# The FFN input product by a Strassen scheme of seven half-token products, and weight tiles moved by 192 bytes

## The chip, the cores and the metric

The kernel runs on one core of one Trainium2 chip. The metric is the device time of one execution in microseconds (us). Engines are named as in the profile: PE is TensorE (its weight loads are listed as PEld), DVE is VectorE, ACT is ScalarE, POOL is GpSimd, SP is the engine that issues the DMAs. All of the data is fp32; matmuls read it as fp32r, in three products of split operands (below).

## The reference

512 tokens of width 1024 pass through eight mixer and FFN blocks: two layers of the form FFN, mixer (an mLSTM in the first, a windowed attention in the second), FFN, with a layer norm after each, and then two layers of a gated mixer and an FFN, with an RMS norm ahead of each. Six FFNs are computed in all, each with 2816 hidden units:

```python
def swiglu(x, w_in, w_out):
    gu = x @ w_in                              # 512 x 1024 by 1024 x 5632
    g, u = gu[..., :D_FF], gu[..., D_FF:]      # D_FF = 2816
    return (jax.nn.silu(g) * u) @ w_out        # 2816 -> 1024
```

The change touches `x @ w_in` in each of these six.

## The kernel before

Activations lie transposed: eight tiles of 128 features by 512 tokens (`xh`, `xl`: the fp32r rounding of x, and the rest). Every weight tile is split in the same way, by `split` (L171 to L177): ACT writes the rounding `wh` (L174), DVE subtracts it from the raw tile and writes `wl` (L177). `mm3` (L202 to L208) then makes a product of three matmuls: x high by w high (L206), x low by w high (L207), x high by w low (L208). Each matmul has a weight load of its own. The weight is the stationary operand (128 by 128), x is the moving one (512 columns, or 256 where tokens are taken by halves HA and HB).

`raw` (L179) loads a weight tile of 128 by 1024 (512 KB) into a ring of three (`wr`); `wh` and `wl` have rings of three as well. All of these tiles start at multiples of 256 bytes within a partition, since `fill` tiles pad the pools to that.

`ffn` (L272) has 22 pairs of hidden tiles, `w_in[m, :, j]` with j = 0 for g and j = 1 for u; one `w_in` tile holds all of K = 1024 for 128 hidden units. `pre` (L216) takes the first four tiles (m = 0, 1), half of the tokens at a time, so that it can begin while the norm before it still works on HB. The norm's work on a half is a generator that `flush(s.start)` (L224) empties ahead of the half's matmuls. `gemms` (L231) then takes the other 40 tiles with 512 moving columns, 24 matmuls a tile, two weight tiles ahead. `gate` (L279 to L284) follows each pair: ACT's silu of g (L281), DVE's product with u (L283), and the split of the result into `hh`, `hl` for the second matmul. `out_gemm` multiplies by `w_out`: `out_head` (L323) takes whole rows of 512 tokens in units of eight, eight and six k-tiles, `out_tail` the last rows by halves, and the norm that follows begins inside that.

The order of instructions in an engine's queue is not that of the program text: the framework's scheduler lays them out when the kernel is built, each engine taking the earliest instruction in the text that is ready by then. The rings and the data set what is ready.

Of the kernel before, what the change touches and what calls it, by code (L numbers as in the profile page):

```python
# [34 lines left out]
AP, AF_, AK = 2, 3, 1  # L35
NP = 4
PACE = 2.0
# [19 lines left out]
class Core:  # L57
    def __init__(self, ctx, tc, consts):
# [127 lines left out]
    def weights(self, src, n=1024, at=None):  # L186

        w = self.raw(src, n)
        if at:
# [12 lines left out]
    def mm3(self, out, w, k, xh, xl, start, stop):  # L202
        mm = self.nc.tensor.matmul
        wh, wl = (a[k // 4][:, k % 4 * 128:k % 4 * 128 + 128] if isinstance(a, tuple) else a[:, k * 128:(k + 1) * 128]
                  for a in w)
# [9 lines left out]

    def pre(self, srcs, ats=()):  # L216

# [53 lines left out]

    def ffn(self, w_in, w_out, half, post, tail=None):  # L272

        nc, tc = self.nc, self.tc
        with tc.tile_pool(name="h", bufs=1) as hp:
            hh = [hp.tile([128, T], F32R, name=f"hh{m}") for m in range(NM)]
            hl = [hp.tile([128, T], F32R, name=f"hl{m}") for m in range(NM)]

            def gate(m, pg, pu):  # L279
                sg = hp.tile([128, T], F32, name="sg", bufs=2)  # L280
                nc.scalar.activation(sg, pg, AF.Silu)  # L281
                hf = hp.tile([128, T], F32, name="hf", bufs=2)
                nc.vector.scalar_tensor_tensor(hf, pu, half, sg, op0=OP.mult, op1=OP.mult)  # L283
                self.split(hh[m], hl[m], hf)  # L284
            first = [(m, j) for m in range(3) for j in range(2)][:NP]
            ats = [tuple(tuple(a[m:m + 2]) for a in (hh, hl)) for m in range(NM - 2, NM - 2 * (NP - 2), -2)]
            p0 = dict(zip(first, self.pre([w_in[m, :, j] for m, j in first], ats)))
            pend = {}

            def cb(m, j):  # L290
                def f(p):
                    pend[j] = p
                    if j:
                        gate(m, pend[0], p)
                return f
            for (m, j), p in p0.items():
                cb(m, j)(p)
            self.run((self.gemms([("a", w_in[m, :, j], cb(m, j)) for m in range(NM) for j in range(2)
                                  if (m, j) not in p0]), 1.0))
            self.out_gemm(w_out, hh, hl, NM, post, tail or FT)  # L300

    def out_gemm(self, w_out, hh, hl, nk, post, tail):

        self.run((self.out_head(w_out, hh, hl, nk, post, KD - tail), 1.0))
        self.out_tail(w_out, hh, hl, nk, post, tail)
# [16 lines left out]

    def out_head(self, w_out, hh, hl, nk, post, head):  # L323
        post.begin(self)
        seq = [(d, (i, min(i + 8, nk))) for d in range(head) for i in range(0, nk, 8)]
        held = {}
        for i, u in enumerate(seq):
# [3 lines left out]
            if i == len(seq) - 1:  # L331
                self.first_tail(w_out, nk, head)
            d, (k0, k1) = u
            if k0 == 0:
                p = self.bank()
# [1184 lines left out]
def program(tc, d, out):  # L1520
    with ExitStack() as ctx:
# [11 lines left out]
        with tc.tile_pool(name="b2t", bufs=1) as S:  # L1533
            c.fill(S, 1216)
# [8 lines left out]
        for l in range(2):  # L1543
            w = {n: d["b_" + n][l] for n in ("hf", "hq", "hg", "c", "hi", "nq", "kk", "vv", "w1", "out", "rope")}
            b2.layer(l, w, RMS(c.k("ffn_g", 8 * l, 8)))
            c.ffn(d["b_win"][l], d["b_wout"][l], 1.0, Out(out) if l else RMS(c.k("mix_g", 8, 8)))

# [127 lines left out]
```

## Time and profile before

| | us |
|---|---|
| median of three runs | 3350.05 (3348.68 to 3352.29) |
| profiled execution, its own time | 3350.13 |
| span of its instructions | 3348.3 |
| PE busy | 3305.9 (99%) |
| DVE busy | 1686.3 (50%) |
| ACT busy | 1280.9 (38%) |
| mean of the DMA queues | 91 GB/s |

A busy time is the sum of an engine's instructions. Matmuls are pipelined, so one that lasts 0.39 us may be followed by the next 0.227 us after its start; the pace is read from starts. In the lists below a row has the start, the time it lasts, the engine, the line, the operation with its tiles (out <- in), and how many were merged into the row. What stands in brackets is the engine's idle time before it and what ended that.

### The profile page before, as it was taken

What the parts mean: (1) busy time and instruction counts of PE and PEld (TensorE: products, weight loads), DVE (VectorE), ACT (ScalarE), POOL (GpSimd) and SP (SyncE); (2) the same over time, 40 slices, a digit from 0 to 9 for tenths busy, and PEclk for the clock granted to TensorE, in tenths of its full rate; (3) what the DMA queues carried; (4) which work ended last, traced back from release to release, by engine and by line L of the source; (5) the groups of instructions that cost most, each with busy time, mean ns of one, the idle gap of its engine ahead of it and who ended that gap; (6) DMA issues with size and microseconds to landing.
All of it is one profiled execution on the core that took longest, in us unless ns stands there. A gap on an engine that the chain in (4) does not pass through costs nothing.

```text
span 3348.3 us, 46248 instructions
## 1 busy us (share of the span) xinstructions
PE 3305.9 (99%) x18704; PEld 2827.0 (84%) x18704; DVE 1686.3 (50%) x3451; ACT 1280.9 (38%) x2231; POOL 96.1 (3%) x138
## 2 busy tenths in 40 slices
PE   8999999999999999999999989999999999999999
PEld 7888977988898888879888978788888988898888
DVE  4333756733354333787334667775333567853332
ACT  3322545522233222685222433563232335632221
POOL 0000011000000000110000000000000000000000
PEclk9999999999999999999999989999999999999999
DMA  4333322233332333212333523112333332023333
GB/s 143 96 94 97 100 76 64 89 97 98 93 109 89 100 94 108 74 41 89 95 98 98 163 88 94 45 51 82 99 95 94 107 115 64 26 72 102 98 101 95
DMA packets 88918, 304.04 MB, mean 91 GB/s; under 512 B 9857, under 2 KB 12417, under 8 KB 88705
## 3 DMA queue, kind: packets, MB, share of 16 engines
q1 hardware_dynamic: 88704, 301.10, 29.3%
q8 instruction: 146, 2.39, 0.3%
q14 instruction: 68, 0.55, 0.0%
HBM read 298.96 MB, written 2.10 MB: 90 GB/s over the span
## 4 chain that ended last, share of the span: by engine, by line
PE 94%; DVE 3%; ACT 2%; DMA 1%; issue 1%; POOL 0%; DVEq 0%; SPq 0%; ACTq 0%; POOLq 0%
PE b L206 26%; PE b L208 26%; PE b L207 26%; PE b L267 2%; PE b L268 2%; PE b L266 2%; PE b L1250 1%; PE b L1442 1%; PE b L1391 1%; PE b L1420 1%; PE b L716 1%; ACT wh L174 1%; DVE wl L177 1%; PE b L1303 1%; DMA wr<-w_in 1%
## 5 line engine op out<-in xcount | busy, mean ns | idle before, releaser
L174 ACT ACTIVATE wh<-wr 128x1024 fp32r<-128x1024 f32 (+3 forms) x532 | 545.0, 1026 | 1568.1 <-PE b L207 980.5
L177 DVE TENSOR_TENSOR wl<-wr,wh 128x1024 fp32r<-128x1024 f32 (+3 forms) x532 | 628.3, 1183 | 867.2 <-ACT wh L174 864.9
L206 PE MATMUL b<-xh,wh 128*128 128x512 f32 (+1 forms) x2712 | 1021.7, 378 | 9.5 <-ACT xh L174 7.4
L208 PE MATMUL b<-xh,wl 128*128 128x512 f32 (+1 forms) x2712 | 1008.8, 373 | 3.2 <-DVE wl L177 3.2
L207 PE MATMUL b<-xl,wh 128*128 128x512 f32 (+1 forms) x2712 | 1008.7, 373 | 2.9 <-DVE xl L177 1.8
L206 PEld LDWEIGHTS b<-xh,wh 128*128 128x128 f32 x2712 | 511.1, 189 | 105.5 <-issue 9.4
L208 PEld LDWEIGHTS b<-xh,wl 128*128 128x128 f32 x2712 | 512.5, 189 | 94.5 <-DVE wl L177 5.8
L207 PEld LDWEIGHTS b<-xl,wh 128*128 128x128 f32 x2712 | 513.1, 189 | 91.7 <-issue 3.5
L206 PE MATMUL b<-hh,wh 128*128 128x512 f32 (+1 forms) x1144 | 400.4, 350 | 0.0
L208 PE MATMUL b<-hh,wl 128*128 128x512 f32 (+1 forms) x1144 | 398.4, 348 | 0.0
L207 PE MATMUL b<-hl,wh 128*128 128x512 f32 (+1 forms) x1144 | 398.3, 348 | 0.0
L283 DVE SCALAR_TENSOR_TENSOR hf<-b,sg 128x512 f32<-128x512 f32 x132 | 90.7, 691 | 407.4 <-PE b L208 404.0
L206 PEld LDWEIGHTS b<-hh,wh 128*128 128x128 f32 x1144 | 216.5, 189 | 28.6 <-issue 1.0
L207 PEld LDWEIGHTS b<-hl,wh 128*128 128x128 f32 x1144 | 216.5, 189 | 28.5 <-issue 1.0
L208 PEld LDWEIGHTS b<-hh,wl 128*128 128x128 f32 x1144 | 216.5, 189 | 27.6
L267 PE MATMUL b<-wl,xh 128*128 128x512 f32 (+2 forms) x352 | 122.8, 349 | 4.3 <-DVE wl L177 4.2
L266 PE MATMUL b<-wh,xh 128*128 128x512 f32 (+2 forms) x352 | 125.1, 360 | 0.0
L268 PE MATMUL b<-wh,xl 128*128 128x512 f32 (+2 forms) x352 | 122.7, 349 | 0.0
L177 DVE TENSOR_TENSOR hl<-hf,hh 128x512 fp32r<-128x512 f32 x132 | 89.9, 685 | 0.0
L174 ACT ACTIVATE hh<-hf 128x512 fp32r<-128x512 f32 x132 | 82.8, 632 | 0.8
L1395 ACT ACTIVATE sc<-sc,nm 128x128 f32<-128x128 f32 (+3 forms) x128 | 71.1, 557 | 23.5 <-DVE nm L1393 22.5
L267 PEld LDWEIGHTS b<-wl,xh 128*128 128x128 f32 x352 | 67.2, 191 | 14.3 <-DVE wl L177 6.1
(408 smaller groups left out, 4122.1 us busy)
## 6 DMA issues: line engine op xcount, KB each, us to landing
wr<-w_in SPq DMA_DIRECT2D x176, 512.0 KB, 3.7
wr<-b_win SPq DMA_DIRECT2D x88, 512.0 KB, 3.7
wr<-w_out SPq DMA_DIRECT2D x80, 512.0 KB, 3.5
wr<-b_wout SPq DMA_DIRECT2D x36, 512.0 KB, 3.5
wr<-w_out SPq DMA_DIRECT2D x36, 384.0 KB, 3.1
wr<-b_out SPq DMA_DIRECT2D x20, 512.0 KB, 3.6
wr<-b_w SPq DMA_DIRECT2D x16, 512.0 KB, 3.8
wr<-b_wout SPq DMA_DIRECT2D x16, 384.0 KB, 3.2
```

The lines of the kernel that those rows point to most:

```text
L174: nc.scalar.activation(h, src, AF.Copy)
L177: nc.vector.tensor_sub(l, src, h.bitcast(F32))
L206: mm(out, wh, xh, start=start, stop=False)
L207: mm(out, wh, xl, start=False, stop=False)
L208: mm(out, wl, xh, start=False, stop=stop)
L266: mm(ps[t][:, :n], self.xh[k][:, ts], wh, start=k == 0, stop=False)
L267: mm(ps[t][:, :n], self.xh[k][:, ts], wl, start=False, stop=False)
L268: mm(ps[t][:, :n], self.xl[k][:, ts], wh, start=False, stop=k == KD - 1)
L283: nc.vector.scalar_tensor_tensor(hf, pu, half, sg, op0=OP.mult, op1=OP.mult)
L716: nc.tensor.matmul(p[:, :257], w[:, (j - j0) * 128:(j - j0 + 1) * 128], v[s][:, h], start=s == ss[0], stop=s == ss[-1])
L1250: nc.tensor.matmul(p[:, i * 64:(i + 1) * 64], K[h][:, ts], q, start=True, stop=True)
L1395: nc.scalar.activation(sc[:, :N], sc[:, :N], AF.Exp, bias=nm[:, g:g + 1], scale=-1.0, accum_out=sm[:, g:g + 1])
```

## The change

Two things change. `ffn` computes the input product of hidden pairs 1 to 10 (a pair is m = 2p and 2p + 1, with its g and its u) by a Strassen-Winograd scheme. K and the tokens are halved, and g and u are the two rows of blocks: seven products stand for eight. One product is `w` (128 hidden units twice, K = 512) by x (K = 512, 256 tokens), 2 x 4 x 3 matmuls of 256 columns, in one PSUM bank. Pair 0 stays with `pre`. The stationary operands of three products are sums of weight blocks, which DVE makes from the raw tiles (`weight`). The moving ones of four products are differences of x blocks (`stage`, made once for each FFN, ahead of `pre`'s HB half; in the last two FFNs x is first put together from `xh + xl` by `whole`). The results are put together in `after`, by DVE adds from PSUM. h stays in fp32 for each pair, and is split for the second matmul at the end (`halves`). Weight reads go over seven raw tiles (three of the ring and four more), in the order of use, with two runs of 2 KB for each partition.

And the rings `wr`, `wh`, `wl` begin 192 bytes past a multiple of 256; 64 bytes behind them bring everything after back to a multiple.

In the diff, `ks` in `stage` are four pieces of 256 columns (one of 1024 in the last two FFNs, `normed`), `put` is a `split` of 1024, `b` in `after` is the product's bank (128 by 512), `whole` is eight adds of 256 for each half where `normed`, and `halves` makes one split of 1024 for each pair of hidden tiles.

```diff
         self.act = ctx.enter_context(tc.tile_pool(name="act", bufs=1))
+        self.fill(ctx.enter_context(tc.tile_pool(name="fill0", bufs=1)), 192)
         self.wraw = ctx.enter_context(tc.tile_pool(name="wraw", bufs=3))
         self.wsp = ctx.enter_context(tc.tile_pool(name="wsp", bufs=3))
+        self.fill(ctx.enter_context(tc.tile_pool(name="fill1", bufs=1)), 64)
...
         for s in (HA, HB):
             self.flush(s.start)
+            if then:
+                then(s)
...
+            def stage():
...
+                for k in ks:
+                    sub(q("t1", k), g("b11", k), g("b12", k))
+                for k in ks:
+                    sub(q("t3", k), g("b22", k), g("b12", k))
+                for k in ks:
+                    stt(q("t2", k), q("t1", k), -1.0, g("b22", k), op0=OP.mult, op1=OP.subtract)
+                put("t2")
+                for k in ks:
+                    stt(q("t4", k), q("t2", k), -1.0, g("b21", k), op0=OP.mult, op1=OP.subtract)
+                put("t3")
+                put("t1")
...
+            def weight(st):
+                p, x = st
+                g = lambda q: raws[p, q]
+                if x == "p6":
+                    held["s2", p] = wide("s2", dt=F32)
+                    nc.vector.tensor_add(held["s2", p], g(0), g(3))
+                elif x == "p5":
+                    nc.vector.tensor_add(g(2), g(2), g(3))
...
+                self.split(wh, wl, src)
+                if x == "p2":
+                    nc.vector.tensor_add(g(0), g(0), g(2))
+                elif x == "p7":
+                    nc.vector.tensor_add(g(1), g(1), held.pop(("s2", p)))
...
+            def product(st, w):
+                p, x = st
+                P[x] = self.bank()
+                for m in range(2):
+                    for k in range(4):
+                        wk = tuple(a[:, m * T + k * 128:m * T + k * 128 + 128] for a in w)
+                        self.mm3(P[x][:, m * 256:m * 256 + 256], wk, None, *moving(x, k), k == 0, k == 3)
...
+            def after(st):
...
+                if x == "p1":
...
+                    nc.scalar.activation(A[p], b, AF.Copy)
+                elif x == "p2":
...
+                    add(G[p], A[p], b)
+                    nc.scalar.activation(G[p], G[p], AF.Silu)
+                elif x == "p6":
+                    add(A[p], A[p], b)
+                elif x == "p7":
...
+                    add(V[p], A[p], b)
+                elif x == "p5":
...
+                    add(A[p], A[p], b)
+                    add(U[p], V[p], b)
+                elif x == "p3":
...
+                    add(a, a, b)
+                    nc.scalar.activation(a, a, AF.Silu)
+                    nc.vector.scalar_tensor_tensor(pairs(h[p])[:, :, HB], pairs(u), -half, pairs(a), op0=OP.mult,
+                                                   op1=OP.mult)
+                elif x == "p4":
...
+                    add(v, v, b)
+                    nc.vector.scalar_tensor_tensor(pairs(h[p])[:, :, HA], pairs(v), -half, pairs(G.pop(p)), op0=OP.mult,
+                                                   op1=OP.mult)
+            steps = [(p, x) for p in (1, 2) for x in ("p1", "p2")]
+            steps += [(p, x) for p in (1, 2) for x in ("p6", "p7", "p5", "p3", "p4")]
+            steps += [(p, x) for p in range(3, NP2) for x in ("p1", "p2", "p6", "p7", "p5", "p3", "p4")]
...
+            def then(s):
+                whole(s)
+                if s is HB:
+                    fetch()
+                    ahead(0, 2)               # weight() of the first two steps
+                    stage()
...
+            for i, st in enumerate(steps):
+                ahead(i, 3)
+                product(st, ready.popleft())
+                after(st)
+                if i == len(steps) - 3:
+                    loaded[units[0]] = self.out_load(w_out, units[0])
+                    halves(5)
+                elif i == len(steps) - 2:
+                    loaded[units[1]] = self.out_load(w_out, units[1])
+                    halves(9)
```

## Rows read from the trace of the kernel before

**Rows 1.** The page, parts 1 and 4: busy times, and the chain that ended last.
```profile
PE 3305.9 (99%) x18704; PEld 2827.0 (84%) x18704; DVE 1686.3 (50%) x3451; ACT 1280.9 (38%) x2231; POOL 96.1 (3%) x138
...
PE 94%; DVE 3%; ACT 2%; DMA 1%; issue 1%; POOL 0%; DVEq 0%; SPq 0%; ACTq 0%; POOLq 0%
```
**Rows 2.** Table by stretch, the third FFN's input: busy of each engine, clock, DMA share, GB/s.
```profile
1018.00:1237.00 219.00, 218.47 (x964) 180.48 (x963) 78.26 (x84) 65.76 (x86) 0.00 (x0) 1.00 0.33 101
```
**Rows 3.** PE in order of time, 512 columns: the first and last of 28 matmuls.
```profile
1039.83 0.39 PE L207 MATMUL b<-xl,wh 128*128 128x512 f32 x1
...
1045.95 0.39 PE L207 MATMUL b<-xl,wh 128*128 128x512 f32 x1
```
**Rows 4.** PE in order of time, 256 columns (`pre`): first and last of 11 matmuls.
```profile
1016.81 0.28 PE L207 MATMUL b<-xl,wh 128*128 128x256 f32 x1
...
1018.01 0.28 PE L208 MATMUL b<-xh,hl 128*128 128x256 f32 x1
```
**Rows 5.** PE in order of time, the second and third matmul of `gemms`.
```profile
1018.58 0.40 PE L207 MATMUL b<-xl,wh 128*128 128x512 f32 x1
...
1019.50 0.50 PE L208 MATMUL b<-xh,wl 128*128 128x512 f32 x1 [0.53 <-DVE wl L177]
```
**Rows 6.** Groups by line and form, DVE and ACT: busy, mean ns | idle before.
```profile
L177 DVE TENSOR_TENSOR wl<-wr,wh 128x1024 fp32r<-128x1024 f32 x466 | 570.4, 1225 | 845.3 <-ACT wh L174 843.2
L283 DVE SCALAR_TENSOR_TENSOR hf<-b,sg 128x512 f32<-128x512 f32 x132 | 90.7, 691 | 407.4 <-PE b L208 404.0 <-ACT sg L281 3.4
...
L174 ACT ACTIVATE wh<-wr 128x1024 fp32r<-128x1024 f32 x466 | 493.1, 1060 | 1424.1 <-PE b L207 884.3 <-issue 435.0 <-PE b L268 64.8
```
**Rows 7.** DVE in order of time, with no idle time between: starts give the pace.
```profile
1019.36 1.28 DVE L283 SCALAR_TENSOR_TENSOR hf<-b,sg 128x512 f32<-128x512 f32 x2
1020.56 1.22 DVE L177 TENSOR_TENSOR wl<-wr,wh 128x1024 fp32r<-128x1024 f32 x1
1021.69 1.29 DVE L177 TENSOR_TENSOR hl<-hf,hh 128x512 fp32r<-128x512 f32 x2
1022.90 1.22 DVE L177 TENSOR_TENSOR wl<-wr,wh 128x1024 fp32r<-128x1024 f32 x1
```
**Rows 8.** DVE in order of time in a layer norm's loop over d.
```profile
985.28 0.42 DVE L464 TENSOR_TENSOR x<-x,b 128x256 f32<-128x256 f32 x1 [2.77 <-PE b L405]
985.74 0.42 DVE L465 TENSOR_TENSOR x<-x,b 128x256 f32<-128x256 f32 x1
986.08 0.41 DVE L464 TENSOR_TENSOR x<-x,b 128x256 f32<-128x256 f32 x1
...
986.86 0.42 DVE L464 TENSOR_TENSOR x<-x,b 128x256 f32<-128x256 f32 x1
987.52 0.42 DVE L471 TENSOR_TENSOR xl<-x,xh 128x256 fp32r<-128x256 f32 x1 [0.24 <-ACT x L469]
```
**Rows 9.** ACT and DVE in order of time: the first weight split of `gemms`.
```profile
1017.13 1.06 ACT L174 ACTIVATE wh<-wr 128x1024 fp32r<-128x1024 f32 x1 [3.50 <-PE b L207]
...
1018.22 1.23 DVE L177 TENSOR_TENSOR wl<-wr,wh 128x1024 fp32r<-128x1024 f32 x1 [4.13 <-ACT wh L174]
```
**Rows 10.** DVE in order of time, the same place in the first and fifth FFN.
```profile
34.27 1.23 DVE L177 TENSOR_TENSOR wl<-wr,wh 128x1024 fp32r<-128x1024 f32 x1 [12.29 <-ACT wh L174]
...
2301.97 1.23 DVE L177 TENSOR_TENSOR wl<-wr,wh 128x1024 fp32r<-128x1024 f32 x1 [10.18 <-ACT wh L174]
```
**Rows 11.** PE in order of time: ten transposes of 128 columns, and the matmul behind.
```profile
1504.28 1.31 PE L911 MATMUL b<-ident,sc 128*128 128x128 f32 x10
1505.35 0.48 PE L206 MATMUL b<-q,wh 128*128 128x512 f32 x1
```
**Rows 12.** The page, part 5: the counts of matmuls with a weight of the ring.
```profile
L206 PE MATMUL b<-xh,wh 128*128 128x512 f32 (+1 forms) x2712 | 1021.7, 378 | 9.5 <-ACT xh L174 7.4
...
L206 PE MATMUL b<-hh,wh 128*128 128x512 f32 (+1 forms) x1144 | 400.4, 350 | 0.0
```

More of the change, by code (lines that the diff above doesn't have):

```diff
@@ L188, in weights @@
         w = self.raw(src, n)
-        if at:
+        if at and not isinstance(at[0], tuple):
+            h, l = at
+            self.split(h[:, :n], l[:, :n], w[:, :n])
+        elif at:
             for i in range(0, n, T):
@@ L270, in gemms, with ffn @@
                 j[3](ps)
-    def ffn(self, w_in, w_out, half, post, tail=None):
+    def ffn(self, w_in, w_out, half, post, tail=None, normed=False):
         nc, tc = self.nc, self.tc
+        NP2 = NM // 2
         with tc.tile_pool(name="h", bufs=1) as hp:
[L276 to L300, printed above, removed]
@@ L302, in out_gemm, with wide, whole @@
-    def out_gemm(self, w_out, hh, hl, nk, post, tail):
-        self.run((self.out_head(w_out, hh, hl, nk, post, KD - tail), 1.0))
+            def wide(name, bufs=1, dt=F32R):
+                return hp.tile([128, 1024], dt, name=name, bufs=bufs)
+            h = [None] * NP2
+            form, staged = {}, {}
+            parts = {"b11": (0, HA), "b12": (0, HB), "b21": (4, HA), "b22": (4, HB)}
+            def whole(s):
+                for i, n in enumerate(parts):
+                    k0, t = parts[n]
+                    if normed and t is s:
+                        staged[n] = wide(f"h{1 + i}", dt=F32)
+                        for k in range(4):
+                            nc.vector.tensor_add(staged[n][:, k * 256:k * 256 + 256], self.xh[k0 + k][:, t].bitcast(F32),
+                                                 self.xl[k0 + k][:, t].bitcast(F32))
@@ new lines, in moving @@
+            def moving(n, k):
+                if n in ("p1", "p2"):
+                    k, s = (k, HA) if n == "p1" else (k + 4, HA)
+                elif n in ("p3", "p4"):
+                    k, s = (k + 4, HB) if n == "p3" else (k, HB)
+                else:
+                    a, b = form[{"p5": "t1", "p6": "t2", "p7": "t3"}[n]]
+                    return a[:, k * 256:k * 256 + 256], b[:, k * 256:k * 256 + 256]
+                return self.xh[k][:, s], self.xl[k][:, s]
+            loads = deque((p, q) for ps in [(1, 2)] + [(p,) for p in range(3, NP2)] for qs in ((0, 1), (2, 3))
+                          for p in ps for q in qs)
@@ new lines, in ffn, with fetch @@
+            slots, raws, n = [None] * 7, {}, [0]
+            def fetch():
+                while loads:
+                    i = n[0] % 7
+                    if slots[i] is not None:
+                        return
+                    p, q = slots[i] = loads.popleft()
+                    w = self.wraw.tile([128, 1024], F32, name="wr") if i < 3 else wide("er", 4, F32)
+                    j, r = divmod(q, 2)
+                    nc.sync.dma_start(w.rearrange("p (m c) -> p m c", m=2),
+                                      w_in[2 * p:2 * p + 2, :, j, r * T:r * T + T].rearrange("m p c -> p m c"))
+                    raws[p, q] = w
+                    n[0] += 1
@@ new lines, in ffn, with ahead @@
+            steps = [(p, x) for p in (1, 2) for x in ("p1", "p2")]
+            steps += [(p, x) for p in (1, 2) for x in ("p6", "p7", "p5", "p3", "p4")]
+            steps += [(p, x) for p in range(3, NP2) for x in ("p1", "p2", "p6", "p7", "p5", "p3", "p4")]
+            ready = deque()
+            def ahead(i, k):
+                while len(ready) < k and i + len(ready) < len(steps):
+                    ready.append(weight(steps[i + len(ready)]))
+            def then(s):
+                whole(s)
+                if s is HB:
+                    fetch()
+                    ahead(0, 2)
+                    stage()
@@ new lines, in ffn @@
+            ats = [(wide(f"h{i}"), wide(f"h{i - 1}")) for i in (10, 8, 6)]
+            ps = self.pre([w_in[m, :, j] for m in range(2) for j in range(2)], ats, then)
+            for k in range(4):
+                self.split(self.xh[k][:, HB], self.xl[k][:, HB], staged["t4"][:, k * 256:k * 256 + 256])
+            hh, hl = [], []
+            pair = wide("hh0"), wide("hl0")
+            for m in range(2):
+                sg = hp.tile([128, T], F32, name="ga", bufs=2)
+                nc.scalar.activation(sg, ps[2 * m], AF.Silu)
+                nc.vector.scalar_tensor_tensor(sg, ps[2 * m + 1], half, sg, op0=OP.mult, op1=OP.mult)
+                for a, o in zip(pair, (hh, hl)):
+                    o.append(a[:, m * T:m * T + T])
+                self.split(hh[m], hl[m], sg)
@@ new lines, in ffn, with halves @@
+            names = [None, "t2h", "t2l", "t3h", "t3l", "t1h", "t1l", "s2"] + ["er"] * 4
+            def halves(k):
+                while len(hh) <= k:
+                    p = len(hh) // 2
+                    a = [wide(n, 4 if n == "er" else 1) for n in (names[p], names[11] if p == 1 else f"h{p - 1}")]
+                    self.split(*a, h[p])
+                    for i, o in zip(a, (hh, hl)):
+                        o.extend(i[:, m * T:m * T + T] for m in range(2))
+            units = [(0, (i, min(i + 8, NM))) for i in (0, 8)]
@@ new lines, in ffn @@
+            loaded = {}
+            for i, st in enumerate(steps):
[8 more added lines that the diff above has]
+                    halves(9)
+            self.out_gemm(w_out, hh, hl, NM, post, tail or FT, loaded, halves)
@@ L305, in out_gemm @@
+    def out_gemm(self, w_out, hh, hl, nk, post, tail, loaded=None, need=None):
+        self.run((self.out_head(w_out, hh, hl, nk, post, KD - tail, loaded, need), 1.0))
         self.out_tail(w_out, hh, hl, nk, post, tail)
```

57 lines of the change are left out of this document (50 added, 7 removed).

## The prediction

> **What bounds the kernel now.** I read the page first. PE is busy for 99% of the span and holds 94% of the chain that ended last; DVE and ACT hold 3% and 2% [rows 1]. So time goes only where PE does less, or waits. Next I took the stretch that is replaced, in the table by stretch. In the third FFN's input PE is busy 218.5 of 219 us, at a granted clock of 1.00 (the 2.4 GHz level), DVE 78 us, ACT 66 us, and the DMA share is 0.33 [rows 2]; the other five look alike. Busy time tells no pace, since matmuls overlap, so I took starts. Matmuls of 512 columns start (1045.95 - 1039.83) / 27 = 0.2267 us apart [rows 3], those of 256 columns (1018.01 - 1016.81) / 10 = 0.120 us apart [rows 4]. Both are 13 ns above what their columns need at 2.4 GHz (213.3 and 106.7 ns). So two matmuls of half the tokens cost 0.240 us for one of 0.2267, and part of what seven for eight gives is lost at once.
>
> **PE's work.** A pair takes 4 tiles x 24 = 96 matmuls of 512 columns before: 96 x 0.2267 = 21.76 us. After, 7 x 24 = 168 of 256 columns: 168 x 0.120 = 20.16 us. That is 1.60 us a pair, and 96.0 us for 10 pairs in 6 FFNs. Matmuls grow by 720 an FFN, to 18704 + 4320 = 23024. The rest (`pre`, `w_out`, the mixers) keeps its count.
>
> The Trainium skill ("TensorE: Matmul & The Clock Gate", Back-to-back issue gap) gives a start-to-start gap of N / 2.4 + 2.5 ns, which would be an estimated 215.8 and 109.2 ns, 2.4 us a pair and 142 us in all. The trace differs, with 226.7 and 120.0, and the sum goes by the trace.
>
> **DVE's work, which is what grows.** Starts with no idle time between give DVE's pace: 1.13 us for 1024 columns, 0.60 for 512 [rows 7], 0.34 for 256 [rows 8]. I take the adds at the price of the subtractions of the same width; the evacuating adds at that of the gate's product, which reads PSUM too and lasts 0.691 [rows 6]. A pair now has seven splits and four weight adds of 1024, and nine operations of 512: 11 x 1.13 + 9 x 0.60 = 17.83 us, 88% of PE's 20.16 (before, 36% [rows 2]). ACT has ten operations, of at most 1.06 us each [rows 6], 10.6 us. So DVE fits, with 2.3 us to spare, if its queue is filled well. A weight tile's slot comes free when its product ends, two products (5.76 us) before the tile that takes the slot is wanted; a split takes 1.06 + 0.03 + 1.23 us [rows 9], with an add ahead some 1.2 more. That fits too.
>
> The queue's order decides. In the text, DVE waits for ACT in the middle of p6, p5 and p3 (an add, then ACT, then DVE again). But the queue isn't in the text's order. In the norm's loop the text has L464, L465, L471 for each d; DVE ran L464 of the third d ahead of the first L471 [rows 8], and between the gate's product and `hl` it ran a whole `wl` [rows 7]. Such waits get filled with other ready work, and I take them at nothing. If they aren't filled, see the second rival.
>
> **The start of each FFN.** Three FFNs follow a layer norm's last tail. There DVE has an idle time of 4.13 us ahead of the first `wl` [rows 9], so it is free 4.0 us before `pre` ends. Into the queue come two splits and an add (3.4), `stage` with 16 x 0.34 + 3 x 1.13 = 8.8, the splits of t4 (1.4) and pair 0's gate (2.4): 16.0 us. With two pairs, whose first two splits and add are counted, DVE has 16.0 + 35.7 - 3.4 = 48.3 us to do, less 4.0 ahead: 44.3 against PE's 40.3. PE must wait at least 4 us; in the text's order 10 (below). I take 6, nearer to the lower end as rows 8 show a filled queue: 18 us for three. The two FFNs behind an RMS norm have 10.2 us of idle time, the first FFN 12.3 [rows 10]. For the former 2.7 us of `whole` come on top and `stage` is 0.9 shorter: 48.3 + 1.8 - 10.1 = 40.0, so 0 to 6; I take 1.5, twice. The first: 0 to 2, I take 0.5. Together 21.5 us. Something comes back: `gemms` began with a wait for `wl`, 0.92 us between starts where 0.23 is the pace [rows 5]. The first weights are now split before `pre` ends, so 0.69 x 6 = 4.1 us are won.
>
> **The end of each input product.** Ten splits of h (11.3 us), four of `w_out` (4.5) and six evacuations (3.6) come into the last three products and the first two units of `w_out`: 19.4 us in 8.6 + 48 x 0.2267 = 19.5. It just fits. Between 0 and two late splits (2.3 us); I take 0.5, for six FFNs 3 us. DMA moves the same bytes in 7% less time, at a share of 0.33 [rows 2], with seven raw tiles ahead: nothing, unless a tile lands more than a pair late.
>
> **The offset.** No row shows a weight tile off a multiple of 256, so I bound it. In `pre` the pace is the same 0.120 whether the weight is of the ring or of an h tile (`hl`, the last of rows 4). The nearest floor is ten transposes of 128 columns, a weight load each, at (1505.35 - 1504.28) / 10 = 0.107 us [rows 11]. So at most 13 ns a matmul are to be won, on all that have a weight of the ring; and I let as much be lost, with less right, since no steady stretch that I read has more than 13 ns over the columns. I take zero.
>
> The Trainium skill ("SBUF — State Buffer", Who interferes with whom) says that PE has two independent read ports, for weights and for moving data, and waits on nobody; by that the offset would do nothing. No run here shows it yet.
>
> **Sum.** -96.0 - 4.1 + 21.5 + 3 = -75.6 us. Against the profiled execution's own 3350.13 (span 3348.3; the median of the runs, 3350.05, is the same) that gives 3275. With the ends of the start and end costs alone the same case reaches from 3262 to 3310.
>
> **Rivals.**
> *The offset takes off part of the 13 ns.* For it: both widths have the same excess, so it hangs on the matmul and its weight load, not on the columns, and transposes run without it [rows 11]. Against it: it is there with any weight tile. In full, 168 x 0.107 = 18.0 us a pair is about DVE's 17.83, so the pair would stop at some 18.6: 60 x 1.56 = 94 us more. Outside the input product (2712 - 1920 + 1144) x 3 = 5808 matmuls have ring weights [rows 12] (1920 of L206 are `gemms` of the FFNs), 75 us at most. End: 3106; half of it gives 3190. Chance 0.20, from 3150 to 3250.
> *DVE's queue binds, and it gets slower.* Place: the waits for ACT within a pair. If nothing fills them, p6 and p5 cost 1.225 + 0.04 + 1.06 + 0.03 - 1.13 = 1.22 us each, p3 some 0.76 for its silu, two splits that stand behind ACT's other work some 0.35 each, a dependent product 0.13: 4.0 us. DVE's pair is then 21.8 us, what PE took before (21.76), and nothing is gained in the pairs. It decides at 2.3 us of waits a pair, where PE begins to wait; from 3.9 the kernel gets slower. At the starts DVE in the text's order reaches the third product's `wl` after 20.2 us, 16.2 past `pre`'s end where PE wants it after 6: 10 us, three times, 6 twice, 2 once: 44 us. With 2.3 x 6 at the ends, 60 x 0.05 in the pairs and 4 won back: 3350 + 44 + 14 + 3 - 4 = 3407. Against it: rows 7 and 8. Chance 0.13.
> *Half filled.* DVE waits for some 3 us a pair: 20.8 us, 0.9 gained for 1.6, and 8 us at the starts after a layer norm: 3310 to 3345. Chance 0.10. With 3.8 us nothing changes: 0.06.
> *The offset costs time.* One third of the 13 ns more, 4.4 ns on 168 x 60 + 5808 matmuls, costs 70 us and undoes the gain (3345); above that it is slower. Chance 0.04.
>
> **How the numbers follow.** The forecast (3262 to 3310) has 0.47, the offset's gain 0.20, half filled 0.10, no change 0.06, slower by DVE's queue 0.13, the offset's loss 0.04, of which all is counted as slower. Faster is 0.77, the same 0.06, slower 0.17 (0.2%, 7 us, is about what a measurement of this kernel can tell from no change). The range from 3160 to 3352 leaves out the slower cases (0.17) and the far end of the offset's gain (0.03).
>
> **What would show it.** PE at 0.120 us a matmul through the products, pairs 20.2 us apart, 23024 matmuls; DVE at 85 to 90% of those stretches and 2500 us or more in all; a wait of PE for `wl` in the first pairs after a layer norm, of 4 to 8 us, and almost none later. A pace below 0.118 is the offset. PE waiting for `wl` in every pair, at p6 or p5, is the second rival. I am wrong if DVE has idle time in front of `wl` while PE waits, if DVE's adds are slower than subtractions, or if the raw tiles come late.

## The result, and the profile after

The changed kernel takes 3261.62 us (median of four, 3258.54 to 3271.83) against 3351.13 us (median of four): a ratio of 0.974 (95% interval 0.9715 to 0.9763). The forecast was 3275. The profiled execution took 3258.70 us, 91.4 less than that of before.

The page after, parts 1 and 4: busy times, and the chain that ended last, as [rows 1].

```profile
PE 3187.7 (98%) x23024; PEld 2919.2 (90%) x23024; DVE 2465.7 (76%) x4371; ACT 1520.8 (47%) x2449; POOL 96.8 (3%) x138
...
PE 86%; DVE 7%; ACT 3%; issue 2%; DMA 2%; POOL 0%; POOLq 0%; SPq 0%; DVEq 0%; ACTq 0%
```

PE is still busy for 98%, with the 23024 matmuls that were expected, but DVE has gone from 3% to 7% of the chain. Next, the table by stretch inside the input products of the second and the third FFN, as [rows 2].

```profile
690.00:838.00 148.00, 148.00 (x1259) 148.00 (x1259) 137.19 (x151) 73.42 (x82) 0.00 (x0) 1.00 0.31 99
1025.00:1174.00 149.00, 149.00 (x1317) 149.00 (x1316) 142.86 (x158) 69.71 (x79) 0.00 (x0) 1.00 0.33 103
```

PE never waits in either, at a granted clock of 1.00. Yet the third FFN starts 1317 matmuls in 149 us where the second starts 1259 in 148. So the pace differs. The first matmul of p6 in two pairs that follow each other, first FFN and third FFN, PE in order of time:

```profile
99.65 0.28 PE L210 MATMUL b<-t2h,wh 128*128 128x256 f32 x1
...
119.43 0.28 PE L210 MATMUL b<-t2h,wh 128*128 128x256 f32 x1
...
1040.67 0.28 PE L210 MATMUL b<-t2h,wh 128*128 128x256 f32 x1
...
1059.71 0.28 PE L210 MATMUL b<-t2h,wh 128*128 128x256 f32 x1
```

A pair takes 19.79 us in the first, second, fifth and sixth FFN (168 matmuls 117.8 ns apart) and 19.04 in the third and fourth (113.3 ns). The forecast had 20.16 (120 ns, [rows 4]). Outside the products, matmuls of 512 columns got slower: the first and the last of 28 in `out_head`, (1206.01 - 1199.83) / 27 = 228.9 ns, where [rows 3] have 226.7.

```profile
1199.83 0.39 PE L211 MATMUL b<-h,wh 128*128 128x512 f32 x1
...
1206.01 0.39 PE L211 MATMUL b<-er,wh 128*128 128x512 f32 x1
```

Then the starts. The table by stretch for the start of the fifth FFN (behind an RMS norm), from some 12 us ahead of the end of its first four tiles, before and after; then PE and DVE rows from the second, in order of time:

```profile
2290.00:2322.00 32.00, 31.47 (x186) 27.64 (x185) 12.66 (x17) 11.93 (x16) 0.00 (x0) 1.00 0.28 83
...
2222.00:2254.00 32.00, 27.68 (x214) 26.98 (x214) 30.81 (x49) 16.13 (x26) 0.00 (x0) 0.89 0.03 9
```

```profile
2240.17 0.39 PE L210 MATMUL b<-xh,wh 128*128 128x256 f32 x1 [1.16 <-ACT wh L175]
...
2242.85 0.58 PE L210 MATMUL b<-t2h,wh 128*128 128x256 f32 x1 [2.18 <-ACT wh L175]
...
2244.64 0.58 PE L212 MATMUL b<-xh,wl 128*128 128x256 f32 x1 [0.99 <-DVE wl L178]
...
2245.23 0.41 PE L211 MATMUL b<-xl,wh 128*128 128x256 f32 x1
2245.44 0.41 PE L212 MATMUL b<-xh,wl 128*128 128x256 f32 x1
...
2259.29 0.39 PE L212 MATMUL b<-t1h,wl 128*128 128x256 f32 x1 [1.50 <-DVE wl L178]
```

```profile
2228.32 1.77 DVE L306 TENSOR_TENSOR h<-xh,xl 128x256 f32<-128x256 f32 x5
...
2256.88 1.23 DVE L379 TENSOR_TENSOR s<-wr 128x1024 f32<-128x1024 f32 x1 [1.66 <-DMA wr<-b_win]
```

DVE is full (30.81 of 32 us; 12.66 in the kernel before, with an idle time of 10.18 us, [rows 10]), PE waits three times in six microseconds, and behind the waits matmuls of 256 columns start 0.21 us apart: the granted clock is at its 1.2 GHz level for 17 of them in this product. A fourth wait, 1.50 us, has another origin: DVE stood idle for 1.66 us until a raw weight tile landed, and its `wl` came late by that. Such idle times of DVE for a raw tile lie at the starts of four of the six FFNs (0.92, 0.21, 1.66 and 0.44 us).

I summed this from the starts of all matmuls: what a start-to-start distance has above the pace of its width, where that is over 0.25 us ("wait"), and what matmuls at the 1.2 GHz level lose. The level of such a sum hangs on the pace that is taken off; what counts below are, above all, the differences between its columns. In us:

| waits and half clock | before | after | after without offset | after without differences of x blocks |
|---|---|---|---|---|
| inside the six input products | 4.2 | 35.2 | 33.3 | 5.8 |
| everywhere else | 74.3 | 87.7 | 83.5 | 86.8 |

With it the 91 us are accounted for: -96.0 (pairs at 120 ns) - 38.1 (the faster pace: 1511 + 3 x 1680 matmuls by 2.22 ns, 169 + 2 x 1680 by 6.67 ns) + 31.0 + 13.4 = -89.7; the rest is the pace outside. So two terms were missed, of opposite sign: a pace that the forecast gave to a rival, and starts twice as dear as forecast.

### The profile page after: what moved, and what is told of

The parts are those of the page before. It is cut to its first block, busy times and chain, and to the rows that moved or that the text cites. A ratio compares the mean times of both kernels' runs of the same rounds, so it can differ in the third digit from the quotient of the medians.

```text
span 3257.0 us, 56333 instructions
## 1 busy us (share of the span) xinstructions
PE 3187.7 (98%) x23024; PEld 2919.2 (90%) x23024; DVE 2465.7 (76%) x4371; ACT 1520.8 (47%) x2449; POOL 96.8 (3%) x138
## 3 DMA queue, kind: packets, MB, share of 16 engines
q1 hardware_dynamic: 119424, 301.10, 29.5%
## 4 chain that ended last, share of the span: by engine, by line
PE 86%; DVE 7%; ACT 3%; issue 2%; DMA 2%; POOL 0%; POOLq 0%; SPq 0%; DVEq 0%; ACTq 0%
PE b L212 23%; PE b L210 23%; PE b L211 23%; PE b L274 2%; PE b L275 2%; PE b L273 2%; PE b L1444 1%; DVE wl L178 1%; PE b L1636 1%; PE b L1585 1%; PE b L1614 1%; PE b L910 1%; ACT wh L175 1%; DMA wr<-w_in 1%; ACT xh L662 1%
## 5 line engine op out<-in xcount | busy, mean ns | idle before, releaser
L175 ACT ACTIVATE wh<-wr 128x1024 fp32r<-128x1024 f32 (+2 forms) x454 | 460.1, 1017 | 747.9 <-PE b L211 532.8
L178 DVE TENSOR_TENSOR wl<-wr,wh 128x1024 fp32r<-128x1024 f32 (+2 forms) x454 | 531.1, 1173 | 353.1 <-ACT wh L175 350.5
L210 PE MATMUL b<-xh,wh 128*128 128x256 f32 (+1 forms) x2520 | 757.9, 302 | 15.6 <-ACT xh L175 7.4
L212 PE MATMUL b<-xh,wl 128*128 128x256 f32 (+1 forms) x2520 | 745.2, 296 | 5.5 <-DVE wl L178 5.4
L211 PE MATMUL b<-xl,wh 128*128 128x256 f32 (+1 forms) x2520 | 743.2, 296 | 3.7 <-DVE xl L178 2.2
L211 PE MATMUL b<-h,wh 128*128 128x512 f32 (+1 forms) x936 | 326.8, 349 | 1.0 <-DVE h L178 1.0
L175 ACT ACTIVATE wh<-er 128x1024 fp32r<-128x1024 f32 x186 | 194.4, 1057 | 154.4 <-PE b L211 93.1
L178 DVE TENSOR_TENSOR wl<-er,wh 128x1024 fp32r<-128x1024 f32 x186 | 225.2, 1221 | 9.1 <-ACT wh L175 9.1
L211 PEld LDWEIGHTS b<-h,wh 128*128 128x128 f32 x936 | 175.8, 188 | 29.2 <-DVE h L178 3.8
L210 PE MATMUL b<-t1h,wh 128*128 128x256 f32 (+1 forms) x584 | 171.3, 293 | 1.0 <-ACT wh L175 1.0
```

The lines of the kernel that those rows point to most:

```text
L175: nc.scalar.activation(h, src, AF.Copy)
L178: nc.vector.tensor_sub(l, src, h.bitcast(F32))
```

## The experiments

### Is it the offset?

My theory was that the 192 bytes alone changed the pace; the rival, that the order of the matmuls did. First the change without the offset:

```diff
-        self.fill(ctx.enter_context(tc.tile_pool(name="fill0", bufs=1)), 192)
-        self.fill(ctx.enter_context(tc.tile_pool(name="fill1", bufs=1)), 64)
```

> The changed kernel without the 192 bytes (the rings start at multiples of 256 again), all else as it is. Theory: the offset alone took the matmuls of the products from 120.0 ns to 117.8 ns (four FFNs) and 113.3 ns (two), which is 1680 x (4 x 2.2 + 2 x 6.7) = 37 us in the six input products; outside of them matmuls of 512 columns pay 2.2 ns for it and those of 256 columns win, which about cancels. So 3296 to 3304 us, pairs 20.16 us apart in all FFNs, and the starts as slow as now. This is also the forecast's own case (3275) with its starts mis-sized by some 21 us. Rival: the faster pace comes from the new order of the matmuls and not from the address: then 3255 to 3270 us, and pairs stay at 19.79 and 19.04 us.

Measured: 3291.07 us (3289.41 to 3292.33), ratio 0.982 (0.9807 to 0.9834); 29.5 us more than with it. The same two matmuls as above, first FFN, PE in order of time; all six FFNs have this distance:

```profile
80.24 0.28 PE L208 MATMUL b<-t2h,wh 128*128 128x256 f32 x1
...
100.40 0.28 PE L208 MATMUL b<-t2h,wh 128*128 128x256 f32 x1
```

20.16 us a pair, as forecast, and 5 us below the range I gave. The rival is out. This run is the forecast's own case, since the forecast gave the offset nothing: 3291 where I had 3275.

Then the kernel before with the same two lines added:

> The kernel before with the 192 bytes alone. Theory: matmuls of 512 columns with a weight of the ring start 228.9 ns apart instead of 226.7, some 9000 of them, +20 us; some 2500 of 256 columns win 2 to 7 ns, -5 to -15 us. So 3355 to 3370 us: slower. Rival one: the offset helps both widths, then 3290 to 3335 us. Rival two: it does nothing here, 3350 us.

Measured: 3363.58 us, ratio 1.0036 (1.0023 to 1.005). First and last of 28 matmuls in an input product, PE in order of time:

```profile
99.73 0.39 PE L210 MATMUL b<-xh,wl 128*128 128x512 f32 x1
...
105.91 0.39 PE L210 MATMUL b<-xh,wl 128*128 128x512 f32 x1
```

228.9 ns: the same offset that makes the 256 columns of the products faster makes 512 columns slower, and by itself it costs the kernel before 12 us.

### What about the offset?

Bare streams of the products' matmuls, with nothing else running:

```diff
+                    w = [t[:, o // 4 + q * 128:o // 4 + q * 128 + 128] for t, o in zip(wt, (dh, dl))]
+                    x = [t[:, dx // 4 + k % 4 * 512:dx // 4 + k % 4 * 512 + cols] for t in xt]
...
+                    mm(p[:, :cols], w[0], x[0], start=k == 0, stop=False)
+                    mm(p[:, :cols], w[0], x[1], start=False, stop=False)
+                    mm(p[:, :cols], w[1], x[0], start=False, stop=k == K - 1)
```

> No part of the reference is computed. Streams of matmuls like those of the products (weight high by x high, weight high by x low, weight low by x high, one bank), 120 of 256 columns or 60 of 512, six streams for each case; between two streams PE waits for an evacuation of a length that differs. The cases: both weight tiles at 0, 32, 64, 96, 128, 160, 192, 224 bytes past a multiple of 256, x at a multiple; x at 192 bytes with weights at 0 and at 192; one of the two weight tiles at 192. Theory one: the offset of the weight tile sets the pace, 120.0 ns at 0 and 113 or 118 at 192 whatever the wait ahead of the stream. Theory two: an offset only lets PE fall into one of two rhythms after a wait, 113.3 or 117.8 ns; then streams of one offset differ from each other, and each keeps its pace to its end. Theory three: what counts is the distance between weight and x addresses; then x at 192 with weights at 192 goes at 120 again.

PE in order of time, the 16th and the 119th matmul (103 apart) of three streams: weights at 0; at 64 bytes; at 64 bytes once more, a repetition later.

```profile
925.70 0.28 PE L1748 MATMUL b<-xa,wa 128*128 128x256 f32 x1
...
938.05 0.28 PE L1749 MATMUL b<-xb,wa 128*128 128x256 f32 x1
...
958.38 0.28 PE L1748 MATMUL b<-xa,wa 128*128 128x256 f32 x1
...
970.05 0.28 PE L1749 MATMUL b<-xb,wa 128*128 128x256 f32 x1
...
1263.01 0.28 PE L1748 MATMUL b<-xa,wa 128*128 128x256 f32 x1
...
1275.14 0.28 PE L1749 MATMUL b<-xb,wa 128*128 128x256 f32 x1
```

That is 119.9, 113.3 and 117.8 ns. From the last half of each stream, in ns (six streams a case):

| weights past 256, x past 256 | 256 columns | 512 columns |
|---|---|---|
| 0, 0 | 120.0 six times | 226.7 six times |
| 192, 192 | 120.0 six times | 226.7 six times |
| 64, 0 | 113.3 five times, 117.8 once | 233.3 |
| 0, 192 | 117.8 five times, 113.3 once | 233.3 |
| 192, 0 | 117.8 six times | 228.9 four times, 233.3 twice |
| one weight tile at 192, x at 0 | 117.8 six times each | not run |
| 32, 128, 160 or 224, x at 0 | 118.3, 118.7, 120.0, 116.7 (once 117.8) | 128: 232.2 to 233.5 |
| 96, 0 | 117.3 or 118.7 | not run |

Theory three holds: what counts is the distance between the addresses of weight and x, within 256 bytes. At distance 0 the pace is the same for both at 0 and both at 192; weights at 64 with x at 0, and weights at 0 with x at 192, which is the same distance modulo 256, show the same two paces, in unlike shares. Theory two holds beside it: at some distances (64, 96 and 224; 192 at 512 columns) PE settles into more than one rhythm, and keeps it to the stream's end. One thing the bare streams don't show: at 192, six of six went at 117.8 ns, while the kernel at 192 has two FFNs at 113.3. What picks the rhythm stays open. That a wait can change it, the kernel shows. In the first FFN it started at 113.3 ns and went on at 117.8 after one wait, to the end (PE in order of time; three matmuls take 0.34 us above the wait, 0.36 below it):

```profile
50.01 0.28 PE L210 MATMUL b<-t1h,wh 128*128 128x256 f32 x1
...
50.35 0.28 PE L210 MATMUL b<-t1h,wh 128*128 128x256 f32 x1
...
54.54 0.39 PE L212 MATMUL b<-xh,wl 128*128 128x256 f32 x1 [1.42 <-DVE wl L178]
54.77 0.28 PE L210 MATMUL b<-xh,wh 128*128 128x256 f32 x1
...
55.13 0.28 PE L210 MATMUL b<-xh,wh 128*128 128x256 f32 x1
```

One FFN at 113.3 instead of 117.8 ns is 1680 x 4.45 = 7.5 us. The runs of the changed kernel lie 13 us apart, those without the offset 3. That the rhythms are behind this spread is likely, not shown: only one execution of each has a trace.

### Other places for the weights

One number changed (64 for 192):

> The changed kernel with the rings 64 bytes past a multiple of 256 instead of 192 (one number). Theory (bare streams and the two-place rings): most FFNs at 19.04 us a pair, 7.5 us less for each that was at 19.79, up to 30 us; matmuls of 512 columns lose, in the bare streams 231 to 233 ns at 64 where 192 gave 229 to 233, 0 to 15 us over some 3300. So 3235 to 3262 us, on the slow side of the ring with two places (3240). Rival: the rhythm is a matter of chance and not of the offset: pairs at 19.79 in about four of six FFNs again, and 3260 to 3275 us.

Measured: 3254.66 us (3250.34 to 3260.74), ratio 0.9718 (0.9702 to 0.9734). Five of six FFNs go at 19.04 us a pair, the second at 19.79; but matmuls of 512 columns with a weight of the ring start 232.7 ns apart on average (230.0 in the changed kernel), and eat a part, some 10 us over 3600. The sixth FFN changes its rhythm in its ninth pair, after a start-to-start distance of only 0.18 us (PE in order of time; above it three matmuls take 0.34 us, below it 0.36):

```profile
3093.20 0.28 PE L211 MATMUL b<-t1l,wh 128*128 128x256 f32 x1
3093.32 0.35 PE L212 MATMUL b<-t1h,wl 128*128 128x256 f32 x1
3093.50 0.28 PE L210 MATMUL b<-t1h,wh 128*128 128x256 f32 x1
```

Then two places in the ring, distance 0 for everything but the products:

```diff
-                wh = self.wsp.tile([128, 1024], F32R, name="wh")
-                wl = self.wsp.tile([128, 1024], F32R, name="wl")
+                wh, wl = self.slots(16)        # one tile of six slots; elsewhere slots(0)
```

> The changed kernel with the ring of split weights at a multiple of 256 for everything but the seven products, which take the same slots 64 bytes further on. Theory (what counts is the distance of weight and x within 256 bytes, and the rhythm that PE falls into after a wait): matmuls of 512 columns are back at 226.7 ns, about 3300 of them, -7 us; those of 256 columns outside of the products go at 120 again, +10 us; in the products the streams with weights at 64 bytes went at 113.3 ns in five of six cases and at 117.8 in one, so four or more of the six FFNs should run at 19.04 us a pair, 7.5 us less for each FFN that was at 19.79: 3235 to 3262 us. Rival: 64 does what 192 did (most FFNs at 19.79), then 3260 to 3272 us. Second rival: beside loaded DVE and ACT the address does other things than in the bare streams; then some pace that neither 113.3, 117.8 nor 120 describes.

Measured: 3249.84 us (3240.62 to 3265.79), ratio 0.9712 (0.9688 to 0.9736). Four FFNs at 19.04 and two at 19.79. In this form the last 64 bytes of a place lie in the next slot, so 16 columns of some weights are overwritten where one use of the ring follows the other. A ring without that:

```diff
+    def slots(self, *offs):
+        i = self.rn % 3 * 2112
+        self.rn += 1
+        return [self.ring[:, i + o:i + o + 1024] for o in offs]
...
+                wh, wl = self.slots(16, 1072)  # products: 64 and 192 bytes past
...
+            h, l = self.slots(0, 1088)         # the rest: multiples of 256
```

> The changed kernel with a ring whose six slots are laid out so that no place runs into the next slot: everything but the seven products takes its weights at a multiple of 256 bytes; the products take the high part 64 bytes past and the low part 192 bytes past one. The output is the reference's. Theory (distance of weight and x within 256 bytes): products at 113.3 or 117.8 ns, by the wait that came last, never at 120; matmuls of 512 columns at 226.7. If three to six FFNs go at 19.04 us a pair: 3228 to 3260 us, below the changed kernel. Rival: with the two parts at unlike distances the streams stay at 117.8, as those with only one part moved did; then all FFNs at 19.79, 3262 to 3272 us.

Measured: 3240.36 us (3239.06 to 3244.9), ratio 0.9676 (0.9662 to 0.9691), 21 us below the changed kernel and the fastest version that leaves nothing out. All six FFNs reach 19.04 (all but the first and third after three slower pairs, in which PE still waits), and matmuls of 512 columns with a weight of the ring start 227.9 ns apart on average (227.7 without the offset). The first matmul of p6 in two pairs of the fifth FFN, PE in order of time:

```profile
2354.53 0.28 PE L213 MATMUL b<-t2h,wring 128*128 128x256 f32 x1
...
2373.57 0.28 PE L213 MATMUL b<-t2h,wring 128*128 128x256 f32 x1
```

Why this mixed pair of distances found the fast rhythm in all six FFNs of the traced execution, I can't say.

### What makes the starts dear?

Theory: DVE's backlog. Without the differences of x blocks in `stage`:

```diff
-                for k in ks:
-                    sub(q("t1", k), g("b11", k), g("b12", k))
...
+                        for k in range(4):
+                            s = slice(k * 256, k * 256 + 256)
+                            self.split(form[n][0][:, s], form[n][1][:, s], g(src[n], k))
```

> The changed kernel without the differences of x blocks at each start: the moving forms are splits of plain x blocks, so the products are not those of the scheme. It takes 16 operations of 256 columns (5.4 us of DVE, less 0.6 for splits in quarters) off DVE ahead of the products of four FFNs and 4 of 1024 columns (4.5 us) off two; PE's matmuls stay the same in number. Theory: the waits at the starts (42 us in all against the kernel before, in the last part of the first four tiles and in the first two pairs) are DVE's backlog, so 3 to 4.7 us go in each of the five later FFNs: 15 to 23 us, 3238 to 3248 us. Rival: the waits there come from the order of the weights' splits and the raw tiles, not from the amount of work: then less than 5 us go.

Measured: 3234.05 us, ratio 0.965 (0.9637 to 0.9663), 27.6 less. The start of the fifth FFN (the same 32 us around the end of its first four tiles), table by stretch:

```profile
2211.00:2243.00 32.00, 30.47 (x255) 29.73 (x255) 30.51 (x48) 18.93 (x28) 0.00 (x0) 1.00 0.13 34
```

PE is busy 30.5 us instead of 27.7 and its clock stays at 1.00. Inside the input products waits and half clock fall from 35.2 to 5.8 us (table above). The total falls by less, because one FFN fewer found the fast rhythm (7.5 us), and still by 4 us more than the range I gave. More goes than the 4.5 to 4.8 us of DVE work for each start: without the backlog the clock doesn't fall either; that t1, t2 and t3 no longer wait for each other may add to it, which this run can't tell apart. So the theory holds inside the products. Outside them the sum hardly moves (86.8 after 87.7, 74.3 before), so the differences of x blocks aren't what PE waits for there, and what it is stays open.

Then only `whole`, in the last two FFNs, moved from DVE to ACT:

```diff
-                            nc.vector.tensor_add(staged[n][:, k * 256:k * 256 + 256], self.xh[k0 + k][:, t].bitcast(F32),
-                                                 self.xl[k0 + k][:, t].bitcast(F32))
+                            nc.scalar.activation(staged[n][:, k * 256:k * 256 + 256], self.xh[k0 + k][:, t].bitcast(F32),
+                                                 AF.Copy)
```

> The changed kernel, where the x blocks of the last two FFNs are put together by ACT, as copies of the high parts alone (the low parts are left out of the differences of blocks), instead of by DVE's sixteen adds. Theory: in these two FFNs the start was mis-sized most, since the adds lie within the norm's loop and push it back; with 16 x 0.335 = 5.4 us less on DVE the waits at these two starts fall from some 10 to some 5 us each: 8 to 12 us less in all, with the other four FFNs as they are. Rival: the norm's loop and `stage` set the start and the adds lie in DVE's gaps: less than 3 us. A change of rhythm (7.5 us for an FFN) is told apart by the distance of the pairs.

Measured: 3257.45 us (3243.27 to 3260.38). The total says little, because in the profiled execution all six FFNs fell into 19.79 us. The two starts say it: waits and half clock inside the fifth and sixth input product are 2.6 and 1.9 us, 8.7 and 7.6 in the changed kernel, 11.8 less, where only work was taken off DVE. With two FFNs fewer in the fast rhythm (15 us more) that is 3 us more in all; the two profiled executions are 1.7 apart. Table by stretch, the fifth FFN, again from 12 us ahead of the end of its first four tiles:

```profile
2235.00:2267.00 32.00, 30.08 (x253) 29.47 (x251) 30.34 (x42) 21.01 (x34) 0.00 (x0) 1.00 0.09 31
```

A cure that failed: the weight sums of p6 and p7 for pairs 1 and 2 on POOL, which is idle there.

```diff
-                    nc.vector.tensor_add(held["s2", p], g(0), g(3))
+                    (nc.gpsimd if p < 3 else nc.vector).tensor_add(held["s2", p], g(0), g(3))
...
-                    nc.vector.tensor_add(g(0), g(0), g(2))
+                    (nc.gpsimd if p < 3 else nc.vector).tensor_add(g(0), g(0), g(2))
```

> The changed kernel with four of the weight sums of 1024 columns (those of p6 and p7 for pairs 1 and 2 of each FFN) on POOL instead of DVE; nothing else changes, the output is the reference's. Theory (the starts wait for DVE's backlog): 4 x 1.13 = 4.5 us less on DVE at each start, and POOL, idle there, has the raw tiles long before p6 wants them; 15 to 25 us less than the changed kernel, 3236 to 3247 us. Rival: POOL's sums take so long (its one row of 384 columns takes 1.2 us, so some 3 us each) that p6 waits for them instead, or DVE's own operations get longer beside them: 3255 to 3275 us.

Measured: 3289.11 us, ratio 0.9821 (0.9808 to 0.9834), 27 us more than the changed kernel, and beyond the range of the rival too. POOL and DVE in order of time, in the norm's loop ahead of the second FFN:

```profile
626.56 2.40 POOL L388 TENSOR_TENSOR wr<-wr,er 128x1024 f32<-128x1024 f32 x1 [3.54 <-DMA er<-w_in]
629.03 3.20 POOL L379 TENSOR_TENSOR s<-wr,er 128x1024 f32<-128x1024 f32 x1
```

```profile
627.05 2.98 DVE L178 TENSOR_TENSOR wl<-wr,wh 128x1024 fp32r<-128x1024 f32 x1
629.96 2.56 DVE L665 TENSOR_TENSOR xl<-x,xh 128x256 fp32r<-128x256 f32 x1
```

A subtraction of 1024 columns takes 2.98 us instead of 1.22, one of 256 2.56 instead of 0.42: the first ends 1.07 us behind POOL's first sum (628.96), the second 0.29 us behind the second (632.23). So DVE stands still while POOL adds and does its own work behind it, and nothing was taken off it. The Trainium skill ("SBUF — State Buffer", Who interferes with whom) says that a DVE instruction with two SBUF inputs contends with a GpSimd instruction that reads SBUF; the rows agree. The 27 us are not all of that: in the profiled execution all six FFNs went at 19.79, which is 15 of the 31 us between the two profiled executions. The rest lies ahead of the products, where the waits and half clock of the 70 us ahead of each come to 41 us in all by a sum like the one above, 21 in the changed kernel; inside the products they are about the same.

### Does DVE's work in a pair fit as forecast?

More of it, by repeating operations: 1.73 us a pair (one sum of 1024, one add of 512), and 3.46 us.

```diff
-                    nc.vector.tensor_add(held["s2", p], g(0), g(3))
+                    for _ in range(2):
+                        nc.vector.tensor_add(held["s2", p], g(0), g(3))
...
                     add(U[p], V[p], b)
+                    add(U[p], V[p], b)
```

> Half of the extra DVE work of the run with more adds: one more sum of 1024 and one more add of 512 from PSUM in each pair, 1.73 us; DVE's pair is 17.83 + 1.73 = 19.56 us by the forecast's prices. Theory (prices hold, the order costs only what it must): FFNs at 117.8 ns keep 19.79 us a pair with almost no wait, and those at 113.3 ns cannot hold 19.04. Rival (as soon as the slack is small, DVE's queue waits for products within the pair and loses some 3 us, as with more adds): pairs of 21 to 23 us in all FFNs, +70 to +170 us.

> The changed kernel with DVE's work in each pair increased by repeating operations (same operands, same result): two more sums of 1024 columns and two more adds of 512 from PSUM, 2 x 1.13 + 2 x 0.60 = 3.46 us by the forecast's prices. Theory: DVE's pair was 17.83 us as forecast, so it becomes 21.3 us and sets the pace: pairs 21.2 to 21.4 us apart in every FFN, PE waiting in every pair, 1.5 us more in 45 pairs at 19.79 or 19.04 and more at the starts, +90 to +130 us. Rival: DVE has more room than that (its adds overlap, or its prices are too high), then pairs stay below 20.6 us; or it had none left (its busy time was 96% of the stretch at 19.04), then pairs are 22 us or more.

Measured: 3365.60 and 3564.33 us, one execution each: 104 and 303 us more than the changed kernel, so the rival came in each, and both theories failed. With 1.73 us more, the first matmul of p7 in two pairs of the first FFN, PE in order of time, and the table by stretch over five pairs:

```profile
104.64 0.38 PE L210 MATMUL b<-t3h,wh 128*128 128x256 f32 x1 [0.44 <-ACT wh L175]
...
126.14 0.39 PE L210 MATMUL b<-t3h,wh 128*128 128x256 f32 x1 [0.43 <-ACT wh L175]
```

```profile
125.00:232.50 107.50, 103.07 (x842) 100.19 (x841) 100.33 (x111) 44.76 (x51) 0.00 (x0) 1.00 0.28 89
```

21.50 us a pair, 1.9 above the 19.56 of work. DVE is idle for 7.2 of 107.5 us, 1.4 us a pair. In the changed kernel it is idle for 1.4 us a pair too, where pairs take 19.79 us (10.8 of 148 us in the table of the second FFN). So most of these 1.4 us isn't room: at 19.04 us a pair DVE does with 0.8, but with more work they stay, as waits (in the rows of one such pair four, of 0.33 to 0.35 us, two for ACT and two for PE). With 3.46 us more, pairs are 24.6 to 26.1 us apart, 25.3 on average, 4.0 above the 21.29 of work. Table by stretch there:

```profile
136.00:161.00 25.00, 22.55 (x163) 22.08 (x164) 20.86 (x24) 8.83 (x10) 0.00 (x0) 0.86 0.27 85
```

DVE is busy 20.86 of 25 us: the prices hold, and the queue loses the rest in waits (four in this stretch: three adds for PE, 2.88, 0.76 and 0.28 us, and one `wl` for ACT, 0.19). That is the size of the forecast's second rival, 4.0 us, but not its mechanism: there DVE waited for ACT, here mostly for PE, whose granted clock has fallen to 0.86 in this stretch behind its own waits. In the changed kernel DVE's waits cost nothing, because they are 0.8 to 1.4 us a pair and fit into what its work leaves.

## Why the prediction came out near, step by step

- **PE's work.** Right: 23024 matmuls, and 20.16 us a pair without the offset. Two other terms were off and nearly cancelled, so that 3275 came so near to 3262 is in part luck.
- **The offset**, taken at zero: wrong, worth 29.5 us. The rival with 0.20 had the mechanism and the bound: of 13.3 ns above the columns it takes 2.2 (four FFNs) or 6.7 (two). The forecast's own sign for it, a pace below 118 ns, is there. Two things in my argument failed. That the pace is the same with a weight of the ring and of an h tile was read from rows in which all tiles lie at multiples of 256; they could not show what an offset does. And I priced both widths alike, while 512 columns lose 2.2 ns by it. By the two independent ports for which I cited the Trainium skill ("SBUF — State Buffer", Who interferes with whom) the offset would do nothing; the measurement decides against that.
- **DVE's work in a pair.** Right: 17.83 us fits, PE never waits in a settled pair at 19.04 us (DVE's busy time, in which operations overlap by a tenth of a microsecond, is 142.86 of 149 us there; 2465.7 in all, for the 2500 that I named as a sign). That 2.3 us were to spare was too kind: 1.73 us more cost 1.71 us a pair against 19.79, since DVE's 1.4 us of idle time a pair stayed.
- **The start of each FFN.** This is the step that failed in size: 21.5 us forecast. Without the offset, against before, by the sum of starts (good to a microsecond or two): the three FFNs behind a layer norm 22.5 (18.4 inside the products, 4.1 ahead of them; forecast 18), the two behind an RMS norm 20.4 (14.6 and 5.7; forecast 3), the first FFN -0.3 (0.5): 42.6 in all. For the RMS norm I took DVE's 10 us of idle time [rows 10] as room. But that room is what is left when the norm's loop is over, and the adds of `whole` lie in the loop and prolong it: in the row of 2228.32 they end some 4 us ahead of the end of `pre`, 2234. I had also counted only eight of the sixteen adds (2.7 us). Taking them off DVE gave 11.8 us back. I also left out what a wait does to the clock: 8.7 of the 33.3 us inside the products.
- **What comes back.** Right: 4.2 us for 4.1; `gemms`' first wait is gone.
- **The end of each input product.** 3 us forecast, none measured: no wait stands in the last products of any FFN. Only where pairs take 19.04 us does the first unit of `w_out` then wait for a late split of h, 1.1 us in the third FFN and in the fourth.
- **DMA.** Right in the settled pairs: a share of 0.31 to 0.33 and no wait for a tile. At the starts it was put at nothing and isn't: DVE waits there for a raw tile in four FFNs, up to 1.66 us (the row of 2256.88), and PE waits 1.50 us behind that one.
- **The sum.** -96.0 - 4.2 + 42.6 = -57.6, to 3292.5 for the profiled execution without the offset (3292.33 measured). The start's 42.6 is itself read from that execution, so this shows that nothing is left over, not that the sum foretells it. The forecast's own case ended 16 us too low, and the offset took 29.5 off.

## What to carry to other kernels

Idle time that a trace shows behind a loop is room only for work that doesn't lie in the loop: put the new operations into the order first, then look for what is left. An engine that is to be at 90% needs its waits counted as well as its work: idle time that stays when a known amount of work is added is no room. And where every operand of before has the same alignment, the trace cannot say what alignment is worth: bound it, and measure it with a bare stream before a layout is fixed, for each width by itself.

## What the runs showed of the hardware

- The pace of a stream of weight loads and matmuls depends on the distance of weight and x addresses within 256 bytes: for 256 columns 120.0 ns at distance 0 and 113.3 or 117.8 at 64 and 192; for 512 columns 226.7 at 0 and 228.9 to 233.5 at 64, 128 and 192.
- At some distances there is more than one lasting rhythm. A wait of PE can change it: one of 1.42 us did in the first FFN, and at 64 bytes a distance of 0.18 us between two starts was enough.
- DVE, subtracting one SBUF tile from another, stands still beside a sum on POOL: 2.98 us for 1.22.
- After several waits close together (1.16, 2.18 and 0.99 us at the start of the fifth FFN) the granted clock was at its lower level for 17 matmuls, 12 to 22 at such starts; matmuls of 256 columns then start 0.213 us apart, with nothing above their columns at 1.2 GHz. Behind the single wait of 1.42 us in the first FFN it stayed at 1.00 (table by stretch):

```profile
50.00:60.00 10.00, 8.58 (x74) 8.38 (x73) 9.15 (x12) 5.04 (x6) 0.00 (x0) 1.00 0.52 158
```
